# Attention outputs two query blocks at a time, and layer 2's modulation sums in layer 1's output projection

## The chip, the core and the metric

The kernel runs on one core of a Trainium2 chip. The metric is the device time of one execution in microseconds (us). Below, PE is the matrix engine, DVE, ACT and POOL are the vector, scalar and GpSimd engines, and SP is the engine whose queue issues most DMAs.

## What is computed

Two layers of a decoder trunk on 1024 tokens of width 1024. Each layer has a modulation of the conditioning vector, an input projection into three branches, and an output projection with a norm and a residual. Cut to what matters here:

```python
mod = jax.nn.silu(c) @ w_mod + b_mod                 # c: (1, D), w_mod: (D, 3 * D)
shift, scale, gate = jnp.split(mod, 3, axis=-1)
h = rmsnorm(x, g_pre) * (1.0 + scale[:, None]) + shift[:, None]
proj = h @ w_in
o_a = sliding_window_attention(a_q, a_k, a_v, sinks) * jax.nn.silu(a_g)   # 16 heads of 64, 4 groups of keys
...
mix = jnp.concatenate([o_a, o_b, o_c], axis=-1)
out = rmsnorm(mix @ w_out, g_post)
return x + gate[:, None] * out
```

Branch B is a gated linear attention and branch C a diagonal state-space model (S5) with a gated linear unit.

## The kernel before

Products run in two float32r parts, so that each weight tile is loaded raw (`wraw`, three buffers), rounded by ACT (`whi`) and its rest taken by DVE (`wlo`, L53), with four buffers for each part. The scheduler of the framework orders each engine's instructions by the order in which the program names them and by when their operands and buffers come free in its own estimate; each engine, and SP's queue of DMAs, then runs in that order, and an instruction that waits holds what is behind it.

A layer is emitted in stages: the input norm, the projections of branch B with the S5 tables, branch B, the attention stage, and the output projection. The function `attention` walks eight pairs of heads by eight blocks of 128 queries, 64 blocks a layer. Each block is a generator, `attn_block`, of three steps that run in three successive iterations: scores and softmax (PE L588, L589, DVE L594 and L603, ACT L599), transposes and split of the probabilities (L609, L53), and products with the values (L619, L620). The last step has one PSUM bank `po` a block. The upper half of its partitions is copied by ACT to `t2` (L622), DVE adds the halves head by head (L626), and for the first six pairs POOL multiplies the gate in (L629). For the last two pairs the sum goes straight to `M`, and the gate follows.

Between the blocks the same loop emits the S5 scans (16 batches, in the first 27 blocks; POOL works in each at L1316 and L1322, DVE at L1315 to L1326), queued projections, and one or two steps of an iterator `side`. In layer 1's attention `side` runs `mod_part` eight times: gate columns of layer 1, parts (0, 4) and (0, 5), and all six parts of layer 2, (1, 0) to (1, 5), where the first number is the layer counted from 0. A part is 512 columns; it has eight steps, each of which loads 128 rows into a `wraw` buffer and adds them, scaled by `c`, to an accumulator: 

```python
            if (l, j) > (1, 2):
                nc.gpsimd.tensor_scalar(...)
```

so that (1, 3) to (1, 5) are summed by POOL (L147, L150), the five others by DVE (L133, L135). A few products with ones then sum over the partitions (L159 or L175). The results of parts (1, 0) to (1, 3), shift and scale, are needed when layer 2's input is normed (`prenorm`); the others, the gates, in the output projection of their own layer.

PSUM has two pools: two banks `pj` for projections and six banks for all else. The function `out_proj` takes layer 1's tokens in groups of three, three and two tiles; for each of 16 slices of 128 rows of `w_out` it loads two weight tiles, splits them and the matching slice of `M` (`mhi`, `mlo`) and runs 18 products (L1472), with a bank for each token tile and half of the columns.

Of the kernel before, what the change touches and what calls it, by code (L numbers as in the profile page):

```python
# [13 lines left out]
F32 = mybir.dt.float32  # L14
# [10 lines left out]
P = 128  # L25
D = 1024
# [9 lines left out]
# parts of M at the end of a layer: heads of branch A in pairs, branch B, branch C  # L36
# [5 lines left out]
class Trunk:  # L42
# [7 lines left out]
    def split(self, hi, lo, src):  # L50
        """hi = src rounded to float32r, lo = src - hi (exact in float32r)."""
        self.nc.scalar.copy(hi, src)  # L52
        self.nc.vector.tensor_tensor(out=lo, in0=src, in1=hi.bitcast(F32), op=ALU.subtract)  # L53
# [31 lines left out]
    def queue(self, name, gen, units=4):  # L85
        """units of products in a generator whose first step is to load; units = 0: no such step."""
        self.q.append([name, gen, units, units > 0])

    def prefetch(self, n=0):
        """emit the loads of the queue's entry n ahead of its products."""  # L90
# [4 lines left out]
    def unit(self):  # L95
        """emit one unit of the queue; False if it is empty."""
# [18 lines left out]
    def finish(self, name=None):  # L115
        """emit the queue up to the end of the named entry, or all of it."""
# [7 lines left out]
    def rstd(self, ss, n, w=1):  # L124
        """(ss / n + EPS) ** -0.5 on a small tile, in place."""
# [12 lines left out]
    def mod_part(self, l, j):  # L138
        """512 columns at a time; j: shift 0, 1, scale 2, 3, gate * g_post 4, 5."""
        nc, i = self.nc, self.i  # L140
        cols = slice(j * 512, (j + 1) * 512)
        acc = self.w2("macc")
        for k in range(KD):
            w = self.wraw()[:, 0:512]
            nc.sync.dma_start(w, i["w_mod"][l, k * P:(k + 1) * P, cols])
            if (l, j) > (1, 2):
# [6 lines left out]
            yield  # L153
        if j < 4:
            bm = self.lp.tile([P, KD], F32, name="bm")
            nc.sync.dma_start(bm[:, 0:4], i["b_mod"][l, cols].rearrange("(k p) -> p k", p=P))
            pm = self.psum("pm")
# [24 lines left out]
    # ---- first layer's input: norm, transpose, modulation, split, by blocks of 256 columns; a_v grows with them  # L182
    def startup(self):
# [5 lines left out]
        # c, b_mod and g_pre with D on partitions  # L189
# [12 lines left out]
        def load(n):  # L202
            """256 rows of 512 columns for shift or scale."""
# [12 lines left out]
        # silu(c) = c * (1 + tanh(c / 2)) / 2  # L216
# [6 lines left out]
        # sums that grow side by side in a bank are one group, opened by a product with zeros  # L223
# [22 lines left out]
        # rows of w_mod whose products run on the tensor engine; the others are summed first  # L246
        direct = (((2, 5), (1, 2, 5)), ((2,), (5,)))

        def mods(b):
            """shift and scale of a half of the columns."""  # L250
# [27 lines left out]
        def prep(b, h):  # L278
            """half of the columns, half of the tokens."""
# [1322 lines left out]
```

## Time and profile before

| | |
|---|---|
| three runs | 1858.48, 1860.26 and 1860.9 us |
| median | 1860.26 us |
| profiled execution | its span is 1860.8 us; no time of its own stands beside it |
| PE busy | 94% of the span |
| DVE busy | 73% |
| ACT busy | 46% |
| POOL busy | 32% |
| mean granted clock of PE | 0.980 of full speed |

Shares are means over stages that differ. On the time axis from the span's start, layer 1's attention stage runs from about 386 to 777 us and layer 2's from about 1302 to 1671 us; layer 1's output projection starts at 777 us. A busy PE row includes the modelled end of each product, so a busy share near one does not by itself say that PE never waits.

### The profile page before, as it was taken

How to read it: one execution, taken by the hardware profiler on the slowest of the kernel's cores; microseconds unless marked ns; L12 is line 12 of the kernel's file. 1: busy time of each engine (PE TensorE's matmuls, PEld its weight loads, DVE VectorE, ACT ScalarE, POOL GpSimd, SP SyncE). 2: the span in 40 equal slices, each digit the busy share in tenths (PEclk: the TensorE clock that was granted, in tenths of full speed). 3: DMA queues.
4: the chain of work that ended last, by engine and by line, in shares of the span. 5: the costliest groups of instructions: out<-in, count | busy, mean ns of one | idle time of the engine just before them, and what ended most of it. 6: DMA issues, size and time to landing. Idle time of an engine off the chain costs nothing.

```text
span 1860.8 us, 28251 instructions
## 1 busy us (share of the span) xinstructions
PE 1749.4 (94%) x9403; PEld 1458.5 (78%) x9403; DVE 1353.2 (73%) x2975; ACT 859.7 (46%) x1973; POOL 589.0 (32%) x1005
## 2 busy tenths in 40 slices
PE   7999799999989989999998999999999899999998
PEld 5987688887777677788778878888878767878876
DVE  6986796579999798647676765954898978873534
ACT  5233333445556565446663242423555656642433
POOL 4279750212343454002217850401323511000100
PEclk7999999999999999999998999999999999999999
DMA  8143402235542322335464432222345111113342
GB/s 308 31 108 125 131 29 74 65 113 171 170 142 69 114 74 76 101 125 184 169 199 95 137 102 57 57 60 65 104 128 150 52 46 41 35 51 134 105 165 101
DMA packets 239385, 198.24 MB, mean 107 GB/s; under 512 B 49596, under 2 KB 195068, under 8 KB 239240
## 3 DMA queue, kind: packets, MB, share of 16 engines
q1 hardware_dynamic: 211640, 172.54, 30.9%
q10 hardware_dynamic: 25536, 16.80, 2.9%
q0 software_dynamic: 2064, 7.11, 1.0%
q8 instruction: 74, 1.21, 0.3%
q14 instruction: 71, 0.58, 0.1%
HBM read 163.13 MB, written 37.46 MB: 108 GB/s over the span
## 4 chain that ended last, share of the span: by engine, by line
PE 61%; DVE 21%; ACT 5%; issue 5%; POOL 4%; DMA 4%; SPq 0%; ACTq 0%; DVEq 0%; POOLq 0%
PE py L1472 14%; PE pj L387 9%; PE pj L389 9%; PE pj L388 9%; DVE wlo L53 2%; PE pj L1472 2%; PE pa L884 2%; PE pj L1370 2%; DVE p L594 2%; DVE pl L53 1%; PE pT L609 1%; PE pj L408 1%; PE pj L410 1%; PE pj L409 1%; DVE p L603 1%
## 5 line engine op out<-in xcount | busy, mean ns | idle before, releaser
L387 PE MATMUL pj<-H,whi 128*128 128x512 f32 x1088 | 442.8, 407 | 10.6 <-DVE M L1386 6.4
L389 PE MATMUL pj<-H,wlo 128*128 128x512 f32 x1088 | 431.7, 397 | 5.5 <-DVE wlo L53 5.5
L388 PE MATMUL pj<-H,whi 128*128 128x512 f32 x1088 | 431.0, 396 | 0.0
L53 DVE TENSOR_TENSOR wlo<-wraw,whi 128x512 fp32r<-128x512 f32 (+1 forms) x320 | 238.6, 765 | 87.2 <-ACT whi L52 86.5
L52 ACT CAST whi<-wraw 128x512 fp32r<-128x512 f32 (+1 forms) x320 | 191.4, 618 | 185.3 <-PE pj L388 108.9
L387 PEld LDWEIGHTS pj<-H,whi 128*128 128x128 f32 x1088 | 207.6, 191 | 56.4 <-DVE M L1386 7.2
L389 PEld LDWEIGHTS pj<-H,wlo 128*128 128x128 f32 x1088 | 207.1, 190 | 54.3 <-DVE wlo L53 7.4
L388 PEld LDWEIGHTS pj<-H,whi 128*128 128x128 f32 x1088 | 207.6, 191 | 40.9 <-issue 1.3
L599 ACT ACTIVATE p<-p,st 128x257 f32<-128x257 f32 (+1 forms) x256 | 125.7, 492 | 153.4 <-DVE st L594 133.4
L53 DVE TENSOR_TENSOR mlo<-M,mhi 128x384 fp32r<-128x384 f32 (+2 forms) x80 | 53.4, 675 | 141.8 <-ACT mhi L52 135.7
L1472 PE MATMUL py<-whi,mhi 128*128 128x512 f32 x448 | 142.4, 397 | 6.6 <-ACT whi L52 3.5
L1472 PE MATMUL py<-wlo,mhi 128*128 128x512 f32 x448 | 144.8, 396 | 0.6 <-DVE wlo L53 0.5
L1472 PE MATMUL py<-whi,mlo 128*128 128x512 f32 x448 | 143.3, 394 | 0.7 <-DVE mlo L53 0.7
L1493 POOL TENSOR_SCALAR yrs<-yss 128x1 f32<-128x1 f32 x16 | 6.7, 418 | 376.5 <-ACT junk L1489 375.4
L52 ACT CAST mhi<-M 128x384 fp32r<-128x384 f32 (+2 forms) x80 | 50.3, 634 | 158.4 <-PE pj L1472 92.7
L594 DVE CUSTOM_DVE_ANT_0 p<-sc,bias,sink 128x256 f32<-128x256 f32 (+1 forms) x256 | 111.4, 463 | 9.2 <-PE sc L589 8.1
L583 POOL COPY p<-sink 128x2 f32<-128x2 f32 x128 | 36.0, 283 | 220.9 <-PE pT L609 102.2
L1472 PEld LDWEIGHTS py<-whi,mhi 128*128 128x128 f32 x448 | 83.1, 188 | 28.9 <-ACT whi L52 6.7
L1472 PEld LDWEIGHTS py<-wlo,mhi 128*128 128x128 f32 x448 | 84.2, 188 | 22.9 <-DVE wlo L53 4.1
L1472 PEld LDWEIGHTS py<-whi,mlo 128*128 128x128 f32 x448 | 84.1, 188 | 20.0 <-DVE mlo L53 1.5
L410 PE MATMUL pj<-wlo,H 128*128 128x256 f32 (+1 forms) x320 | 92.9, 292 | 6.3 <-DVE wlo L53 6.3
L408 PE MATMUL pj<-whi,H 128*128 128x256 f32 (+1 forms) x320 | 93.6, 293 | 3.7 <-DVE hv L346 2.7
(380 smaller groups left out, 3931.8 us busy)
## 6 DMA issues: line engine op xcount, KB each, us to landing
wraw<-in_w_in_dram SPq DMA_DIRECT2D x160, 256.0 KB
wraw<-in_w_out_dram SPq DMA_DIRECT2D x160, 256.0 KB
wraw<-in_w_mod_dram SPq DMA_DIRECT2D x64, 256.0 KB
M<-s5tab SPq DMA_DIRECT2D x32, 256.0 KB
M<-s5turn SPq DMA_DIRECT2D x64, 128.0 KB
M<-in_w_mod_dram SPq DMA_DIRECT2D x10, 512.0 KB
s5tab<-O ACTq DMA_DIRECT2D x8, 512.0 KB
s5tab<-G ACTq DMA_DIRECT2D x8, 512.0 KB
```

Source lines behind the costliest of these rows:

```text
L52: self.nc.scalar.copy(hi, src)
L53: self.nc.vector.tensor_tensor(out=lo, in0=src, in1=hi.bitcast(F32), op=ALU.subtract)
L387: nc.tensor.matmul(pj, hi, hh, start=(k == 0), stop=False)
L388: nc.tensor.matmul(pj, hi, hl, start=False, stop=False)
L389: nc.tensor.matmul(pj, lo, hh, start=False, stop=(k == KD - 1))
L408: nc.tensor.matmul(pj[:, :N], hh, hi, start=(k == 0), stop=False)
L410: nc.tensor.matmul(pj[:, :N], hh, lo, start=False, stop=(k == KD - 1))
L594: nc.vector.tensor_tensor_reduce(out=p[:, h, 0:n], in0=sc[:, h * 256:h * 256 + n], in1=bias[:, h, o0:o0 + n], scale=-1.0, scalar=self.sink ...
L599: nc.scalar.activation(p[:, h, 0:n + 1], p[:, h, 0:n + 1], AF.Exp, bias=neg[:, h:h + 1], scale=-1.0, accum_out=den[:, h:h + 1])
L884: nc.tensor.matmul(pa[:, j * P:(j + 1) * P], X[:, c * P:(c + 1) * P], xq[:, :, c * 64:(c + 1) * 64], start=True, stop=True)
L1370: nc.tensor.matmul(pz, wg[:, k, :], self.M[:, MIX_C[k], ts_], start=(k == 0), stop=(k == 3))
L1472: self.nc.tensor.matmul(py[t, h], lhs, ws[h][w][:, 0, :], start=(n == 0 and first), stop=(n == N - 1 and last))
```

## The change

Blocks of queries are taken in twos. An even block's products go to the first half of bank `po` and stop there; the odd block's go to the second half, and then one copy of 64 x 512, two additions of 64 x 256 and one gate multiplication of 128 x 256 serve both. The bank is thus held from the even block's third step to the odd block's.

Modulation parts: layer 1's attention keeps (0, 4), (0, 5) and takes (1, 3) third; all three are summed by POOL, as `pool` is true by default. Parts (1, 0) and (1, 1) on DVE and (1, 2) on POOL run in layer 1's output projection, with raw tiles, accumulators and a PSUM bank of their own (`mraw`, two buffers for both chains; `macc`; `pj`). Parts (1, 4) and (1, 5) run on POOL in layer 2's attention, which had none. The diff also deletes comments; that is left out here.

```diff
-    def mod_part(self, l, j):
+    def mod_part(self, l, j, pool=True, room=None, bank="pm"):
...
-        acc = self.w2("macc")
+        acc = room.tile([P, 512], F32, name="macc") if room else self.w2("macc")
         for k in range(KD):
-            w = self.wraw()[:, 0:512]
+            w = room.tile([P, 512], F32, name="mraw", bufs=2) if room else self.wraw()[:, 0:512]
             nc.sync.dma_start(w, i["w_mod"][l, k * P:(k + 1) * P, cols])
-            if (l, j) > (1, 2):
+            if pool:
...
-            pm = self.psum("pm")
+            pm = self.psum(bank)
...
-        po = self.psum("po")
+        if b % 2 == 0:
+            self.po = self.psum("po")
+        po = self.po
+        dst = po[:, b % 2 * 256:b % 2 * 256 + 256]
         for kt in range(nk):
...
-        t2 = self.ap.tile([64, 256], F32, name="t2", bufs=1)
-        nc.scalar.copy(t2, po[64:128, 0:256])
-        m = self.M[:, MIX_A[pair], b * P:(b + 1) * P]
-        o = self.ap.tile([P, P], F32, name="o") if pair < 6 else m
+        if b % 2 == 0:
+            return
+        t2 = self.ap.tile([64, 512], F32, name="t2", bufs=1)
+        nc.scalar.copy(t2, po[64:128, :])
+        m = self.M[:, MIX_A[pair], (b - 1) * P:(b + 1) * P]
+        o = self.ap.tile([P, 2 * P], F32, name="o") if pair < 6 else m
...
+        side = [] if last else [
+            chain(*(self.mod_part(l + 1, j, False, self.sp, "pj") for j in range(2))),
+            self.mod_part(l + 1, 2, True, self.sp, "pj")]
...
+                if side:
+                    for f in (side[0], side[1], side[0])[:2 + n % 2]:
+                        next(f, None)
...
-            parts = [(0, 4), (0, 5), (1, 0), (1, 1), (1, 2), (1, 3), (1, 4), (1, 5)] if l == 0 else []
+            parts = [(0, 4), (0, 5), (1, 3)] if l == 0 else [(1, 4), (1, 5)]
```

How the instructions move is shown at three places. First, SP's queue of DMAs where layer 1's output projection begins (`wraw` are raw weights, `mraw` raw modulation weights, `gg` the gate, `x_sb` the residual). Before:

```order
L370 DMA wraw<-in_w_out_dram 128x512 x6
L1433 DMA gg<-gg_84 128x1024
L1478 DMA x_sb<-in_x_dram 128x1024 x2
L370 DMA wraw<-in_w_out_dram 128x512 x30
L1501 DMA xmid<-yn 128x1024
```

And now:

```order
L372 DMA wraw<-in_w_out_dram 128x512 x7
L1442 DMA gg<-gg_84 128x1024
L145 DMA mraw<-in_w_mod_dram 128x512 x2
L1494 DMA x_sb<-in_x_dram 128x1024
L145 DMA mraw<-in_w_mod_dram 128x512 x2
L372 DMA wraw<-in_w_out_dram 128x512 x2
L1494 DMA x_sb<-in_x_dram 128x1024
L145 DMA mraw<-in_w_mod_dram 128x512 x2
L372 DMA wraw<-in_w_out_dram 128x512 x2
L145 DMA mraw<-in_w_mod_dram 128x512 x2
L372 DMA wraw<-in_w_out_dram 128x512 x2
```

After the first seven weight loads, two modulation loads now stand ahead of every two weight loads, through twelve such rounds.

Second, POOL at the first S5 scans of layer 1's attention (`s5a<-s5a` and `s5a<-s5b` are the scans' two multiplications, `M<-M,o` the gate, `macc` the modulation sums). Before:

```order
L1316 TENSOR_TENSOR s5a<-s5a,M 128x256
L583 COPY p<-sink 128x2
L1322 TENSOR_TENSOR s5a<-s5b,M 128x256
L1316 TENSOR_TENSOR s5a<-s5a,M 128x256
L1322 TENSOR_TENSOR s5a<-s5b,M 128x256
L583 COPY p<-sink 128x2
L629 TENSOR_TENSOR M<-M,o 128x128
```

And now:

```order
L147 TENSOR_SCALAR wraw<-wraw,cc 128x512
L1325 TENSOR_TENSOR s5a<-s5a,M 128x256
L150 TENSOR_TENSOR macc<-macc,wraw 128x512
L585 COPY p<-sink 128x2
L1331 TENSOR_TENSOR s5a<-s5b,M 128x256
L1325 TENSOR_TENSOR s5a<-s5a,M 128x256
L147 TENSOR_SCALAR wraw<-wraw,cc 128x512
L150 TENSOR_TENSOR macc<-macc,wraw 128x512
L1331 TENSOR_TENSOR s5a<-s5b,M 128x256
L585 COPY p<-sink 128x2 x2
L638 TENSOR_TENSOR M<-M,o 128x256
```

Modulation work of two instructions now stands between the scans' multiplications, where POOL had none of it.

Third, DVE at the start of the output projection, in the change:

```order
L53 TENSOR_TENSOR mlo<-M,mhi 128x384 x3
L133 TENSOR_SCALAR macc<-mraw,cc 128x512
L53 TENSOR_TENSOR mlo<-M,mhi 128x384
L53 TENSOR_TENSOR wlo<-wraw,whi 128x512 x2
L135 SCALAR_TENSOR_TENSOR macc<-mraw,cc,macc 128x512
```

The sums of parts (1, 0) and (1, 1) stand between the splits of the weights and of `M`; before, the splits followed each other alone.

## Rows read from the trace of the kernel before

**Rows 1.** The page, part 1: busy time, share of the span, instructions.

```profile
PE 1749.4 (94%) x9403; PEld 1458.5 (78%) x9403; DVE 1353.2 (73%) x2975; ACT 859.7 (46%) x1973; POOL 589.0 (32%) x1005
```

**Rows 2.** Score reduction L594 by stretch: count, durations (min/median/max), first and last start.

```profile
L594 DVE CUSTOM_DVE_ANT_0 p<-sc,bias,sink x48: 340/478/485, 386.8 to 536.6; 128x256 f32<-128x256 f32 x42, 128x128 f32<-128x128 f32 x6
L594 DVE CUSTOM_DVE_ANT_0 p<-sc,bias,sink x80: 332/479/486, 542.9 to 759.3; 128x256 f32<-128x256 f32 x70, 128x128 f32<-128x128 f32 x10
L594 DVE CUSTOM_DVE_ANT_0 p<-sc,bias,sink x48: 342/478/485, 1302.5 to 1447.2; 128x256 f32<-128x256 f32 x42, 128x128 f32<-128x128 f32 x6
L594 DVE CUSTOM_DVE_ANT_0 p<-sc,bias,sink x80: 339/479/486, 1454.9 to 1653.3; 128x256 f32<-128x256 f32 x70, 128x128 f32<-128x128 f32 x10
```

**Rows 3.** Output projection's products L1472, layer 1 (without its last tiles), then layer 2.

```profile
L1472 PE MATMUL py<-whi,mhi x256: 387/395/505, 777.1 to 967.0; 128*128 128x512 f32 x128
L1472 PE MATMUL py<-whi,mhi x192: 388/393/502, 1671.1 to 1850.0; 128*128 128x512 f32 x192
```

**Rows 4.** Busy time by stretch: length, PE, PEld, DVE, ACT, POOL, PE clock, DMA, GB/s.

```profile
386.00:543.00 157.00, 147.04 (x850) 126.87 (x849) 147.61 (x409) 84.48 (x228) 47.59 (x82) 0.99 0.48 145
543.00:777.00 234.00, 217.48 (x1083) 171.93 (x1083) 196.82 (x526) 133.07 (x338) 88.97 (x133) 0.98 0.30 88
777.00:842.00 65.00, 64.62 (x278) 52.25 (x279) 30.47 (x50) 26.24 (x49) 0.00 (x0) 1.00 0.42 142
1302.00:1455.00 153.00, 145.22 (x845) 125.47 (x843) 137.36 (x387) 86.39 (x233) 49.01 (x84) 1.00 0.41 120
1455.00:1671.00 216.00, 207.92 (x1047) 164.63 (x1047) 174.25 (x499) 129.54 (x333) 40.40 (x85) 0.98 0.15 43
```

**Rows 5.** Modulation sums: DVE from 386 to 543 us; then POOL and PE, all.

```profile
L135 DVE SCALAR_TENSOR_TENSOR macc<-wraw,cc,macc x18: 722/746/753, 387.8 to 542.2; 128x512 f32<-128x512 f32 x18
L133 DVE TENSOR_SCALAR macc<-wraw,cc x3: 457/481/482, 431.5 to 541.7; 128x512 f32<-128x512 f32 x3
...
L150 POOL TENSOR_TENSOR macc<-macc,wraw x21: 1267/1287/2009, 631.1 to 729.9; 128x512 f32<-128x512 f32 x21
L159 PE MATMUL pm<-ones,macc x32: 164/250/250, 526.9 to 665.9; 128*128 128x1 f32 x32
```

**Rows 6.** Output of the blocks: additions, copy, gate, both layers.

```profile
L626 DVE TENSOR_TENSOR o<-po,t x192: 253/283/286, 401.6 to 1590.9; 64x128 f32<-64x128 f32 x192
L622 ACT COPY t<-po x128: 353/370/373, 399.5 to 1664.2; 64x256 f32<-64x256 f32 x128
L629 POOL TENSOR_TENSOR M<-M,o x96: 452/462/966, 402.7 to 1591.4; 128x128 f32<-128x128 f32 x96
```

**Rows 7.** Nearest operations with 256 or 512 columns, on DVE, ACT and POOL.

```profile
L1315 DVE TENSOR_TENSOR s5a<-pe,M x32: 413/422/425, 392.0 to 1447.6; 128x256 f32<-128x256 f32 x32
L52 ACT CAST ph<-pT x128: 365/587/593, 393.5 to 1660.2; 128x512 fp32r<-128x512 f32 x112, 128x256 fp32r<-128x256 f32 x16
L1316 POOL TENSOR_TENSOR s5a<-s5a,M x32: 725/742/989, 391.7 to 1444.2; 128x256 f32<-128x256 f32 x32
```

**Rows 8.** Instructions in time: start, us, engine, line; then all of L603.

```profile
718.74 0.70 POOL L147 TENSOR_SCALAR wraw<-wraw,cc 128x512 f32<-128x512 f32 x1
719.52 1.28 POOL L150 TENSOR_TENSOR macc<-macc,wraw 128x512 f32<-128x512 f32 x1
721.61 1.30 POOL L150 TENSOR_TENSOR macc<-macc,wraw 128x512 f32<-128x512 f32 x1
...
719.65 2.02 DVE L603 TENSOR_SCALAR p<-p,st 128x256 f32<-128x256 f32 x2
721.59 0.67 DVE L1409 SCALAR_TENSOR_TENSOR sgate<-sgate,pj 128x512 f32<-128x512 f32 x1
...
L603 DVE TENSOR_SCALAR p<-p,st x256: 261/350/1467, 388.6 to 1655.1; 128x256 f32<-128x256 f32 x112, 128x128 f32<-128x128 f32 x16
```

**Rows 9.** DVE's waits in layer 2's attention: who for whom, us, times, longest.

```profile
DVE s5a L1317 <- POOL s5a L1316: 3.3, 8, 0.5
```

**Rows 10.** Chain of waits: start, us, what.

```profile
627.55 2.67 DMA wraw<-in_w_mod_dram
...
942.85 4.34 DMA wraw<-in_w_out_dram
```

**Rows 11.** SP's issues of `w_out` from 783 to 801 us; DVE's weight splits there.

```profile
L370 SPq DMA_DIRECT2D wraw<-in_w_out_dram x10: 327/328/328, 783.4 to 800.7; - x10
...
786.88 1.30 DVE L53 TENSOR_TENSOR wlo<-wraw,whi 128x512 fp32r<-128x512 f32 x2
791.04 1.29 DVE L53 TENSOR_TENSOR wlo<-wraw,whi 128x512 fp32r<-128x512 f32 x2
```

More of the change, by code (lines that the diff above doesn't have):

```diff
@@ L153, in mod_part @@
             yield
+        if room:
+            yield
         if j < 4:
@@ L618, in attn_block @@
             sl = slice(kt * 256, (kt + 1) * 256)
-            nc.tensor.matmul(po[:, 0:256], v, ph[:, sl], start=(kt == 0), stop=False)
-            nc.tensor.matmul(po[:, 0:256], v, pl[:, sl], start=False, stop=(kt == nk - 1))
-        t2 = self.ap.tile([64, 256], F32, name="t2", bufs=1)
-        nc.scalar.copy(t2, po[64:128, 0:256])
-        m = self.M[:, MIX_A[pair], b * P:(b + 1) * P]
-        o = self.ap.tile([P, P], F32, name="o") if pair < 6 else m
+            nc.tensor.matmul(dst, v, ph[:, sl], start=(kt == 0), stop=False)
+            nc.tensor.matmul(dst, v, pl[:, sl], start=False, stop=(kt == nk - 1))
+        if b % 2 == 0:
[4 more added lines that the diff above has]
+        o = self.ap.tile([P, 2 * P], F32, name="o") if pair < 6 else m
+        heads = lambda t, h: t.rearrange("p (b h t) -> p b h t", b=2, h=2)[:, :, h, :]
         for h in range(2):
-            nc.vector.tensor_tensor(out=o[64 * h:64 * h + 64, :],
-                                    in0=po[0:64, h * P:(h + 1) * P], in1=t2[:, h * P:(h + 1) * P], op=ALU.add)
+            nc.vector.tensor_tensor(out=o[64 * h:64 * h + 64, :].rearrange("p (b t) -> p b t", b=2),
+                                    in0=heads(po[0:64, :], h), in1=heads(t2, h), op=ALU.add)
         if pair < 6:
```

## The prediction

> **What bounds the kernel now.** I read the page's busy shares first: PE is busy for 94% of the span and DVE for 73% [rows 1]. These are means over unlike stages, so the second step is the places that the change touches, by the first and last starts of one instruction. Layer 1's attention begins with its first score reduction at 386.8 us and ends where the output projection's first product starts, at 777.1; layer 2's runs from 1302.5 to 1671.1 [rows 2, 3]. That is 390.3 against 368.6 us for the same blocks, scans and projections: layer 1 takes 21.7 us more, and what it does more is the eight modulation parts. The trace of before thus holds its own comparison, and the forecast hangs on it.
>
> The score reductions split the surplus. The first three pairs are 48 reductions, and the fourth begins at 542.9 and at 1454.9 [rows 2]: 156.1 against 152.4 us there (3.7 more), 234.2 against 216.2 in the rest (18.0 more).
>
> Third, busy time by stretch [rows 4]. In the first three pairs, where the scans run, DVE is busy for 147.61 of 157 us in layer 1 and for 137.36 of 153 in layer 2. It is nearly full, but the 10.25 us that layer 1 has more cost only 3.7: each us of DVE work there costs 0.36 us of time. That is my rate for DVE work in these stages. PE is close behind (145.22 of 153), and this limits what a lighter DVE can return. In the output projection PE is busy for 64.62 of 65 us, DVE for half, POOL not at all: modulation hides there only while nothing delays PE's weights.
>
> **The change part by part.**
>
> A. Layer 1's pairs 3 to 7 lose all modulation: the last DVE parts, and the three POOL parts whose 21 additions run from 631.1 to 729.9 us [rows 5]. The price is the 18.0 us between the layers. I take -17, since some of it may be chance in how the two layers fall; the bounds are -18 and half, -9.
>
> B. The first three pairs lose 18 x 0.746 + 3 x 0.48 = 14.9 us of DVE sums [rows 5], and get about 21 steps on POOL, each 0.70 + 1.29 = 2.0 us [rows 5, 8]. These are not free to DVE. While POOL worked on such steps without a break, two multiplications L603 on DVE took 2.02 us together, where one alone has a median of 0.35; a gate operation L1409 that reads PSUM took 0.67 beside a full 1.30 us POOL addition [rows 8]. So an operation of one kind pays (1.3 us over one and a half steps, up to 0.9 a step) and others pay nothing. I take 0.4 a step: 8.4 us back, a net 6.5 us less on DVE, by 0.36 some -2.3. The scans' multiplications on POOL now stand behind modulation; DVE's wait for them is small now (3.3 us in eight waits [rows 9]), and I add 0.8. Sum -1.5; bounds -5 (the 14.9 at 0.36, nothing back) and +5 (0.9 a step, and some 3 us of waits).
>
> On this point the Trainium skill is stricter. Its page "SBUF — State Buffer", section "Who interferes with whom", says that DVE and GpSimd share a port pair as an exclusive lock for a whole instruction, where DVE has two SBUF inputs or runs in a two-port mode. The longer L603 and the untouched L1409 agree with it. Taken to its end it gives the slow rival below; by the rows the sum goes on with 0.4.
>
> C. Outputs of two blocks together, 32 times a layer. DVE: four additions of 0.283 become two. The nearest row for twice the columns from PSUM is L1315, 0.422, so 1.13 becomes 0.84: 0.29 x 32 = 9.2 us less a layer. ACT: two copies of 0.370 become one, near 0.587 (512 columns from PSUM), 4.9 us less. POOL: two gates of 0.462 become one of 0.742 (256 columns), 0.18 x 24 = 4.4 us less [rows 6, 7]. ACT and POOL have room, so only DVE's share counts: 9.2 x 0.36 = 3.3 a layer, for both -6. Bounds: 0, if the bank that is held longer makes PE wait, and -18.4, if DVE's time counts in full. PE's own products stay.
>
> D. Layer 2's attention gets parts (1, 4) and (1, 5) on POOL: 16 steps x 0.4 x 0.36 = 2.3, and 0.7 for the scans' waits, +3. Bounds 0 and +8 (0.9 a step is 5.2, and some 3 us of waits). Two gate products move along, at nothing.
>
> E. The 12 small products of parts (1, 0) to (1, 2) move into a stage that PE fills: 12 x 0.11 to 0.25 us [rows 5], +1.5 (1.3 to 3). The 16 sums on DVE, 12 us, have room in a stage in which DVE is idle for over 30 of 65 us.
>
> F. The 24 loads of these parts stand in SP's queue ahead of weight loads, two by two, and share two buffers. The next pair waits until both are used, and the weights queue behind it. A load that POOL uses takes 0.33 to issue and 2.67 to land [rows 10, 11], then 2.0 us of POOL: 5.0, where PE needs two weight tiles each 18 products; weights are split every 4.16 us (786.88 to 791.04 [rows 11]). DVE's loads take 0.33 + 2.67 + 0.75 = 3.75 and keep up. With twice the traffic a landing may take 3.2, so a POOL round takes 5.5 and loses 1.3. POOL uses eight of the 24 loads; where two in turn fall on one buffer the whole round is lost, elsewhere part of it. I count four to eight full losses, 5 to 10 us. Against this stands the lead: weights issued at 783.4 land near 786.1, PE needs them as its fourth slice, at 777.1 + 3 x 4.16 = 789.6 [rows 3, 11], and the split takes 0.65 on DVE and about as much on ACT before: some 2.2 us to spare, and for the pair's second tile, needed 4.16 later, some 6. What is left is 0 to 7; I take +3. With the landing of 4.34 of a busier stretch [rows 10] it would be +12, the upper bound.
>
> **Sum:** -17 - 1.5 - 6 + 3 + 1.5 + 3 = -17. Everything else keeps its instructions. The profiled execution's span is 1860.8, half a us above the median of the runs, 1860.26; the forecast is 1860.8 - 17 = **1844 us**.
>
> **The rivals.**
>
> 1. *DVE's time counts in full.* In the scans it is 94% to 95% busy, which speaks for it; that 10.25 us cost only 3.7 speaks against it. A -18, B -6.5, C -18.4, D +6.4, E and F +4.5: -32, 1829 us.
>
> 2. *The output projection starves* behind modulation loads: F is +12 in place of +3, 1853 us. For it: PE has no idle time there now, so any late weight shows at once. Against: the lead, and loads that land in 2.67.
>
> 3. *The change doesn't give what it says.* The bank is held for a block longer, PE waits for it and C is 0; B is 0, and half of A was never modulation's: -9 + 3 + 4.5 = -1.5, 1859 us. Against: six banks remain for at most two or three users at once.
>
> 4. *Slower: POOL's modulation holds DVE in the scans.* POOL gets 21 + 16 steps where DVE is fullest. If each held DVE for its whole 2.0 us, as the skill's lock would have it at worst, 37 x 2.0 x 0.36 = 26.6 would stand for the 5.3 that I count: +21, 1865 us. The forecast turns into a loss when a step costs over about 1.7 us of DVE, for 37 x 0.36 x (1.7 - 0.4) = 17. For it: L603 at three times its median. Against: the dense stretch shows at most 0.9, and L1409 nothing.
>
> **How the numbers follow.** The forecast's case, 1837 to 1851, gets 0.60; rival 1 0.12, rival 2 0.10, rival 3 0.10, rival 4 0.08. The range 1828 to 1858 takes in rivals 1 and 2 and the forecast's bounds, and leaves out rival 4 and part of 3. About 0.2%, 3.7 us, is what a measurement can tell from no change, so faster means below 1856.5: the forecast, rivals 1 and 2, 0.82. Within 0.2% is rival 3, 0.10; slower is rival 4, 0.08.
>
> **What would show it.** In the changed profile the two attention stages should take nearly the same time, each near 365 to 370 us, and layer 1's pairs 3 to 7 should take near 214 us (A). The pair additions should take 0.42 us, 128 in place of 256 (C). L603 should be longer beside POOL's sums in the first pairs, and by how much decides rival 4 (B, D). In the output projection PE's busy share in the first 65 us, and SP's waits for POOL's additions, decide F; if that first group of tiles takes over 72 us, rival 2 holds. The forecast is wrong if layer 1's attention stays over 380 us, or layer 2's goes over 376.

## The result, and the profile after

The changed kernel took 1882.8 us (median of four runs, 1881.81 to 1884.57), the one before 1860.58 beside it: a ratio of 1.0126, 95% interval [1.0113, 1.014]. The forecast was 1844, so the sign was wrong. The profiled execution of the changed kernel has a span of 1881.8 us, 21.0 more than before. Lines moved: the score reduction is now L596, the products of the output projection L1488, the scans' POOL multiplications L1325 and L1331.

The page's busy times, against [rows 1]: DVE works 33.9 us less, POOL 35.9 more.

```profile
PE 1753.2 (93%) x9403; PEld 1459.9 (78%) x9403; DVE 1319.3 (70%) x2823; ACT 847.8 (45%) x1909; POOL 624.9 (33%) x1002
```

The score reductions of the changed kernel by stretch (count; shortest, median and longest ns; first and last start), as [rows 2]:

```profile
L596 DVE CUSTOM_DVE_ANT_0 p<-sc,bias,sink x48: 343/478/486, 388.1 to 552.2; 128x256 f32<-128x256 f32 x42, 128x128 f32<-128x128 f32 x6
L596 DVE CUSTOM_DVE_ANT_0 p<-sc,bias,sink x80: 338/478/485, 558.8 to 755.7; 128x256 f32<-128x256 f32 x70, 128x128 f32<-128x128 f32 x10
L596 DVE CUSTOM_DVE_ANT_0 p<-sc,bias,sink x48: 343/479/485, 1310.6 to 1470.3; 128x256 f32<-128x256 f32 x42, 128x128 f32<-128x128 f32 x6
L596 DVE CUSTOM_DVE_ANT_0 p<-sc,bias,sink x80: 337/478/486, 1477.9 to 1674.9; 128x256 f32<-128x256 f32 x70, 128x128 f32<-128x128 f32 x10
```

The output projection's first token tiles (96 products of one kind a group of three tiles), two groups before, then two of the changed kernel:

```profile
L1472 PE MATMUL py<-whi,mhi x96: 390/394/501, 777.1 to 843.2; 128*128 128x512 f32 x96
L1472 PE MATMUL py<-whi,mhi x96: 388/394/482, 844.3 to 912.4; 128*128 128x512 f32 x96
```

```profile
L1488 PE MATMUL py<-whi,mhi x96: 386/393/506, 773.8 to 850.0; 128*128 128x512 f32 x96
L1488 PE MATMUL py<-whi,mhi x96: 387/394/483, 851.2 to 919.2; 128*128 128x512 f32 x96
```

Differences of first starts give the account. Layer 1's first three pairs take 170.7 us (388.1 to 558.8) and took 156.1: +14.6. Its pairs 3 to 7 take 215.0 (to 773.8) and took 234.2: -19.2. The first three tiles take 77.4 and took 67.2: +10.2. Layer 2's first three pairs take 167.3 and took 152.4: +14.9. These four make +20.5 of the 21.0. So the modulation left pairs 3 to 7 as forecast, and cost more at each of the three places that it went to.

Busy time by stretch of the changed kernel (columns as in [rows 4]): the first three pairs, the rest and the first tiles, then the first three pairs of layer 2.

```profile
388.00:559.00 171.00, 150.03 (x843) 129.75 (x842) 145.09 (x371) 85.62 (x222) 83.07 (x111) 0.96 0.47 138
559.00:774.00 215.00, 207.68 (x1060) 165.04 (x1059) 168.99 (x457) 125.06 (x312) 38.79 (x74) 0.99 0.15 43
774.00:851.00 77.00, 72.86 (x312) 55.60 (x312) 47.70 (x73) 28.70 (x56) 17.96 (x17) 1.00 0.63 207
1310.00:1478.00 168.00, 150.90 (x849) 129.66 (x848) 140.49 (x369) 85.36 (x222) 68.09 (x96) 0.96 0.43 129
```

In the first three pairs DVE is busy for 145.09 of 171 us: it works less than before and stands idle for 26 us in place of 9. It is not a full DVE that makes the stage longer. PE stands idle for 21 in place of 10, and its granted clock is 0.96 in place of 0.99. Who waits for whom there (us in total, times, longest; `s5a` are the scans' intermediate sums), before and after:

```profile
DVE s5a L1317 <- POOL s5a L1316: 0.8, 3, 0.4
PE py L1332 <- DVE s5a L1326: 6.2, 6, 1.8
```

```profile
POOL wraw L147 <- DMA wraw<-in_w_mod_dram: 13.7, 7, 2.9
DVE s5a L1326 <- POOL s5a L1325: 12.0, 4, 6.5
PE py L1341 <- DVE s5a L1335: 17.3, 8, 7.3
```

POOL waits for modulation loads, DVE waits for POOL's first scan multiplication, PE waits for the end of the scan. The timeline shows one such chain at the start of layer 2's attention (start, us, engine, line; in brackets the idle time before and what the profile takes for its releaser):

```profile
1316.35 0.69 POOL L147 TENSOR_SCALAR wraw<-wraw,cc 128x512 f32<-128x512 f32 x1 [3.79 <-DVE s5a L1324]
1317.13 1.29 POOL L150 TENSOR_TENSOR macc<-macc,wraw 128x512 f32<-128x512 f32 x1
1321.31 0.69 POOL L147 TENSOR_SCALAR wraw<-wraw,cc 128x512 f32<-128x512 f32 x1 [2.90 <-DMA wraw<-in_w_mod_dram]
1321.97 0.72 POOL L1325 TENSOR_TENSOR s5a<-s5a,M 128x256 f32<-128x256 f32 x1
1322.72 1.47 DVE L1326 TENSOR_TENSOR s5a<-s5a 128x256 f32<-128x256 f32 x1 [6.86 <-POOL s5a L1325]
1328.68 0.80 PE L1341 MATMUL py<-s5a,M 128*128 128x127 f32 x2 [7.66 <-DVE s5a L1335]
```

L1325 multiplies what ACT copies out of PSUM in L1322 and L1323, and the second copy ends at 1315.4. POOL stands at a modulation step then, whose load lands at 1316.1 (the profile names L1324 there, which the step does not read). L1325 comes behind it and behind half of the next one: 1.98 us of sums, 2.90 of waiting for the next load, 0.69 of the next step. DVE, in order too, idles for 6.86 us, and then PE for 7.66. PE pays a second time, as busy time by stretch around that stop shows (the columns of [rows 4], with the clock behind POOL's):

```profile
1315.00:1321.00 6.00, 6.00 (x33) 4.94 (x31) 0.64 (x3) 2.63 (x8) 1.98 (x2) 1.00 0.23 75
1321.00:1328.60 7.60, 0.02 (x1) 0.00 (x0) 5.80 (x12) 0.00 (x0) 5.87 (x8) 0.70 0.12 35
1328.60:1334.00 5.40, 5.32 (x21) 4.93 (x22) 5.17 (x18) 3.12 (x9) 2.22 (x3) 0.50 0.47 139
```

After standing for 7.6 us PE runs at half its clock (1.2 GHz, the lower of its two levels) for the next 5.4 us.

### The profile page after: what moved, and what is told of

Read it like the earlier page. It is cut to its first block, busy times and chain, and to the rows that moved or that the text cites. A ratio compares the mean times of both kernels' runs of the same rounds, so it can differ in the third digit from the quotient of the medians.

```text
span 1881.8 us, 28019 instructions
## 1 busy us (share of the span) xinstructions
PE 1753.2 (93%) x9403; PEld 1459.9 (78%) x9403; DVE 1319.3 (70%) x2823; ACT 847.8 (45%) x1909; POOL 624.9 (33%) x1002
## 5 line engine op out<-in xcount | busy, mean ns | idle before, releaser
L601 ACT ACTIVATE p<-p,st 128x257 f32<-128x257 f32 (+1 forms) x256 | 125.7, 493 | 176.6 <-DVE st L596 168.4
L1488 PE MATMUL py<-whi,mhi 128*128 128x512 f32 x448 | 144.0, 399 | 7.9 <-ACT whi L52 4.6
L1488 PE MATMUL py<-wlo,mhi 128*128 128x512 f32 x448 | 147.8, 401 | 1.2 <-DVE wlo L53 0.8
L1488 PE MATMUL py<-whi,mlo 128*128 128x512 f32 x448 | 144.0, 395 | 0.7 <-DVE mlo L53 0.7
L585 POOL COPY p<-sink 128x2 f32<-128x2 f32 x128 | 34.4, 270 | 293.8 <-PE pT L611 162.4
L596 DVE CUSTOM_DVE_ANT_0 p<-sc,bias,sink 128x256 f32<-128x256 f32 (+1 forms) x256 | 111.5, 463 | 20.1 <-PE sc L591 19.1
L1488 PEld LDWEIGHTS py<-whi,mhi 128*128 128x128 f32 x448 | 83.0, 188 | 31.5 <-ACT whi L52 9.7
L1488 PEld LDWEIGHTS py<-wlo,mhi 128*128 128x128 f32 x448 | 84.8, 189 | 26.9 <-DVE wlo L53 8.8
L1488 PEld LDWEIGHTS py<-whi,mlo 128*128 128x128 f32 x448 | 84.8, 190 | 19.6 <-DVE mlo L53 1.5
```

Of the source, the lines that this page charges most:

```text
L585: nc.gpsimd.tensor_copy(p[:, :, n], self.sink[:, h0:h0 + 2])
L596: nc.vector.tensor_tensor_reduce(out=p[:, h, 0:n], in0=sc[:, h * 256:h * 256 + n], in1=bias[:, h, o0:o0 + n], scale=-1.0, scalar=self.sink ...
L601: nc.scalar.activation(p[:, h, 0:n + 1], p[:, h, 0:n + 1], AF.Exp, bias=neg[:, h:h + 1], scale=-1.0, accum_out=den[:, h:h + 1])
L1488: self.nc.tensor.matmul(py[t, h], lhs, ws[h][w][:, 0, :], start=(n == 0 and first), stop=(n == N - 1 and last))
```

## The experiments

Below, "first three pairs" is layer 1's and layer 2's stretch from the first score reduction to that of the fourth pair, "pairs 3 to 7" the rest up to the output projection, "first tiles" the first group of three; all are differences of first starts in one profiled execution, as above. Ratios are to the kernel before, run on the same chip (medians of 1861.7 to 1864.0 there).

| kernel | time, us | ratio, interval | first three pairs | pairs 3 to 7 | first tiles |
|---|---|---|---|---|---|
| before | 1860.58 | | 156.1, 152.4 | 234.2, 216.2 | 67.2 |
| changed | 1882.8 | 1.0126 [1.0113, 1.014] | 170.7, 167.3 | 215.0, 215.3 | 77.4 |
| pairing alone | 1865.36 | 1.0018 [0.9999, 1.0037] | 153.8, 149.5 | 239.1, 215.2 | 67.2 |
| moves alone | 1885.89 | 1.0133 [1.0112, 1.0155] | 172.5, 169.4 | 215.7, 215.8 | 77.1 |
| DVE sums in attention | 1854.07 | 0.9955 [0.994, 0.9971] | 156.0, 153.8 | 215.0, 215.3 | 78.7 |
| steps from block 4 | 1880.11 | 1.0101 [1.0072, 1.0129] | 171.1, 165.4 | 217.4, 215.0 | 78.6 |
| steps from block 28 | 1894.28 | 1.0172 [1.0145, 1.0198] | 148.5, 148.1 | 249.9, 237.9 | 78.2 |
| no loads | 1862.9 | 0.9999 [0.9979, 1.002] | 162.3, 155.2 | 215.7, 214.8 | 79.4 |
| small sums | 1848.51 | 0.9928 [0.9904, 0.9952] | 154.8, 154.7 | 215.5, 215.2 | 78.7 |
| loads by POOL | 1916.48 | 1.0283 [1.0245, 1.032] | 192.6, 178.8 | 214.5, 215.0 | 78.0 |
| own raw tile | 1881.18 | 1.0099 [1.0057, 1.0142] | 173.2, 163.8 | 214.4, 215.2 | 79.3 |
| block 28, loads by POOL | 1892.9 | 1.0167 [1.0109, 1.0224] | 148.5, 148.6 | 250.9, 232.8 | 77.7 |
| projection on DVE | 1880.23 | 1.0085 [1.0062, 1.0108] | 171.9, 166.7 | 215.0, 215.5 | 73.9 |
| four raw tiles | 1878.25 | 1.0084 [1.0054, 1.0115] | 172.2, 166.9 | 216.2, 215.3 | 75.5 |
| all sums on DVE | 1855.39 | 0.9947 [0.9925, 0.9968] | 157.9, 155.2 | 215.3, 215.1 | 72.9 |
| all in attention, DVE | 1854.16 | 0.9948 [0.9932, 0.9964] | 153.7, 155.3 | 225.1, 214.9 | 67.2 |
| all on DVE, own tile | 1860.53 | 0.9999 [0.9981, 1.0018] | 162.1, 157.3 | 215.6, 215.1 | 72.2 |

The stage columns repeat well where the code is the same: layer 2's pairs 3 to 7 take 214.8 to 215.8 us in the fourteen kernels whose steps do not reach them, the first tiles 77.1 to 79.4 in the ten that leave them as in the changed kernel, and layer 1's first three pairs 170.7 to 172.2 in three. Smaller differences than these say nothing.

**Which half of the change.** Pairing alone takes the moves back, by the edit below; moves alone keeps one bank, copy and gate a block.

```diff
-        side = [] if last else [
+        side = [] and [
...
-            parts = [(0, 4), (0, 5), (1, 3)] if l == 0 else [(1, 4), (1, 5)]
-            self.attention(l, (s for a in parts for s in self.mod_part(*a)))
+            parts = [(0, 4), (0, 5), (1, 0), (1, 1), (1, 2), (1, 3), (1, 4), (1, 5)] if l == 0 else []
+            self.attention(l, (s for a in parts for s in self.mod_part(*a, a > (1, 2))))
```

> The changed kernel's pairing of blocks alone; all eight modulation parts stand where the kernel before had them (five on DVE, three on POOL, all in layer 1's attention). Theory Q (order: in the changed kernel the first S5 multiplication on POOL stands behind eight modulation steps that load one at a time, and DVE and PE wait for it): without those steps the first three pairs take 150 to 157 us in both layers, as before, and the whole 1850 to 1860 us. Theory L (POOL's modulation slows DVE through a shared resource, step by step): the same numbers. Theory B (a bank held for two blocks makes PE wait): the first three pairs stay near 171 and 167 us as in the changed kernel, and the whole is 1880 us or more.

> The changed kernel's modulation moves alone; each block has its own bank, copy, additions and gate as before. Q and L: the first three pairs stay at 165 to 171 us in both layers, the output projection's first three tiles at 75 to 79 us (67 before), the whole 1878 to 1892 us. B: the first three pairs return to 152 to 158 us, the whole below 1865 us.

Pairing gives 2.3 and 2.9 us in the first three pairs and in layer 2's rest 1.0; in layer 1's rest, where modulation runs as before, it takes 4.9 more. As a whole it cannot be told from no change, and misses the 1850 to 1860 us expected. The moves alone are as slow as the whole change. So the bank held for two blocks (theory B) is not the cause; the moves are.

**Which engine.** The sums of both attention stages go to DVE, in the same places.

```diff
-            self.attention(l, (s for a in parts for s in self.mod_part(*a)))
+            self.attention(l, (s for a in parts for s in self.mod_part(*a, False)))
```

> The changed kernel with the five parts in the two attention stages summed by DVE instead of POOL, in the same places of the program. Q: the first scan is free again; first three pairs 153 to 160 us in both layers, the whole 1853 to 1863 us (the output projection keeps its 10 us). L: the same direction, as POOL has no steps there. B: no change against the changed kernel, 1880 us.

The stages fall back by 14.7 and 13.5 us, and the time is below both kernels. A step works DVE, the fuller engine, for 0.75 us, and yet costs less time than on POOL. So it is POOL's steps in these stages that cost; what remains is how.

**Where in the stage.** The steps start with block 4, behind the first scan.

```diff
-                for _ in range(2 if n % 6 == 0 else 1):
+                for _ in range((2 if n % 6 == 0 else 1) if n >= 4 else 0):
```

> The changed kernel with the attention's modulation steps begun four blocks later, still on POOL and still within the scans, so that no step stands ahead of the first two scans' multiplications. Q: most of the first pair's 10 to 12 us comes back in each layer; first three pairs 154 to 162 us, the whole 1858 to 1870 us. L: the same 24 and 16 steps slow DVE by as much as before, first three pairs 165 to 172 us, the whole 1878 to 1886 us.

The narrow form of theory Q fell: the sum stays, the loss only moves on to the later pairs, and the numbers are those of theory L. (All 24 and 16 steps now lie in the first three pairs; in the changed kernel four in each layer stand ahead of the first score reduction, which leaves 20 and 12.) The loss also has another form here. In layer 1's first three pairs DVE's wait for POOL's first multiplication, and two of its own operations (busy, mean ns, idle), are

```profile
DVE s5a L1326 <- POOL s5a L1325: 4.9, 10, 1.2
L605 DVE TENSOR_SCALAR p<-p,st 128x256 f32<-128x256 f32 (+1 forms) x48 | 20.2, 462 | 0.5
L1329 DVE TENSOR_TENSOR_SCAN s5b<-rho,s5a 128x128 f32<-128x128 f32 x32 | 16.4, 544 | 0.2
```

The wait is 4.9 us in place of 12.0, and DVE is busy for 151.93 us in place of 145.09: its operations are longer. The means of the two were 346 and 413 ns in the kernel before.

So the next question was whether scans are needed for the loss at all; with 28 in place of 4 the steps come after the last one.

> The changed kernel, but the modulation steps in both attention stages begin with block 28 (after the last S5 scan) in place of block 0; they stay on POOL, with the same loads. Theory Q2 (POOL's steps cost because the scans stand among them on POOL and DVE: without a scan to hold, a step is free): the first three pairs fall from 170.7 to about 153 and from 167.3 to about 150 us, as where nothing or only DVE sums stand there, pairs 3 to 7 stay at 215 to 218, and the time falls by 28 to 34 us to 1849 to 1855. Theory L2 (each POOL step slows DVE by its port wherever it stands; 1.0 us of time a step): the first three pairs fall as above, but pairs 3 to 7 rise by as much, 24 and 16 us, to 239 and 231, and the time stays near 1880.

The first three pairs come out at 148.5 and 148.1 us, the measure for this stage without any modulation. But pairs 3 to 7 pay more than the scans did: 249.9 and 237.9 in place of 215, about 1.4 us for each of the 24 and 16 steps. So theory Q2 fell, and theory L2's 1.0 us a step was too little. The rows on ACT in layer 1 (who for whom, us, times, longest):

```profile
ACT whi L52 <- DMA wraw<-in_w_in_dram: 17.9, 2, 11.1
ACT ge L1360 <- POOL ge L1359: 13.1, 7, 4.1
```

Two holders show: input weights that arrive late behind modulation loads, and POOL's part of the S5 gate. To tell them apart, POOL issues the loads into a tile of its own, so that SP's queue no longer sees them (here and in the other kernels with a tile of their own, `o` has one buffer, which is left out below):

```diff
-            w = room.tile([P, 512], F32, name="mraw", bufs=2) if room else self.wraw()[:, 0:512]
-            nc.sync.dma_start(w, i["w_mod"][l, k * P:(k + 1) * P, cols])
+            w = room.tile([P, 512], F32, name="mraw", bufs=2) if room else self.ap.tile([P, 512], F32, name="mraw", bufs=1)
+            (nc.sync if room else nc.gpsimd).dma_start(w, i["w_mod"][l, k * P:(k + 1) * P, cols])
```

> The changed kernel, with the modulation steps of the attention stages begun at block 28, after the scans, and their loads issued by POOL into a raw tile of their own. It tells apart why the late steps cost 34.9 and 22.8 us in pairs 3 to 7. Theory S (there by SP: the input projection's weights stand behind modulation loads whose raw tile POOL still holds): pairs 3 to 7 fall from 249.9 to 215 to 224 and from 238.0 to 215 to 220 us, and the time is 1846 to 1856. Theory H (POOL's own waits hold the gates and the gelu behind it, there too): they stay at 235 to 265 and 228 to 245.

The waits for `w_in` fall to 1.9 us, and the stage stays long (250.9 and 232.8), as theory H had it. POOL's own queue holds it:

```profile
POOL mraw L147 <- DMA mraw<-in_w_mod_dram: 35.3, 16, 3.1
ACT p L601 <- POOL p L585: 20.4, 5, 7.8
ACT ge L1360 <- POOL ge L1359: 18.2, 8, 5.9
```

L585 is POOL's copy of the sink into each block's scores, 0.19 us long in the median, and every exponent L601 on ACT needs it. POOL was 32% busy in the kernel before, but it has an operation on the path of every block.

**Load or sum.** One kernel keeps POOL's arithmetic and leaves seven of eight loads out; the other keeps all loads and cuts the sums to 16 columns (the multiplication in the same way as the addition below). Neither computes the whole modulation.

```diff
-            w = room.tile([P, 512], F32, name="mraw", bufs=2) if room else self.wraw()[:, 0:512]
-            nc.sync.dma_start(w, i["w_mod"][l, k * P:(k + 1) * P, cols])
+            if room or k == 0:
+                w = room.tile([P, 512], F32, name="mraw", bufs=2) if room else self.wraw()[:, 0:512]
+                nc.sync.dma_start(w, i["w_mod"][l, k * P:(k + 1) * P, cols])
+            else:
+                w = acc
```

> The changed kernel, but in the attention stages only the first step of a modulation part loads its weights; the other seven repeat the two POOL operations of a step on the accumulator itself, in the same shapes. This leaves out seven eighths of these parts' weights, so the modulation is not the reference's. POOL's arithmetic stays, its waits for loads and their places in SP's queue go. Without loads to wait for, the scheduler places a part's steps closer together. Theory A (the 2.0 us of POOL arithmetic a step, which hold the scans' POOL multiplications and lengthen DVE's operations): the first three pairs stay at 163 to 171 and 160 to 167 us. Theory W (POOL stands at the head of its queue for a load of 2.9 us, and the raw tiles hold SP's queue): they fall to 154 to 158 and 150 to 154.

```diff
+                c = slice(0, 16 if k and not room else 512)
...
-                    nc.gpsimd.tensor_tensor(out=acc, in0=acc, in1=w, op=ALU.add)
+                    nc.gpsimd.tensor_tensor(out=acc[:, c], in0=acc[:, c], in1=w[:, c], op=ALU.add)
```

> The changed kernel, but in the attention stages POOL's two operations of a modulation step take 16 of the 512 columns (the first step of each part stays whole). This leaves out most of these sums, so the modulation is not the reference's. Every load, its place in SP's queue and POOL's order of instructions stay as in the changed kernel; of the 2.0 us of arithmetic a step some 0.2 should be left. Theory A (the arithmetic costs): the first three pairs fall from 170.7 to 153 to 158 and from 167.3 to 149 to 154 us. Theory W (the waits for the loads cost, with POOL's and SP's queues behind them): they stay above 164 and 161. Between these, the two share it, and the part that each has is read from this run and the one without loads.

The waits of DVE and PE in layer 1's first three pairs, without loads, then with small sums:

```profile
DVE s5a L1329 <- POOL s5a L1328: 5.0, 4, 3.8
PE py L1344 <- DVE s5a L1338: 13.1, 8, 5.1
```

```profile
DVE s5a L1327 <- POOL s5a L1326: 1.6, 4, 0.4
PE py L1342 <- DVE s5a L1336: 4.6, 4, 1.9
```

Over the 148.5 and 148.1 of a stage without modulation, sums alone cost 13.8 and 7.1, loads alone 6.3 and 6.6, both together 22.2 and 19.2. These hold different numbers of steps, as the scheduler puts some ahead of the first score reduction: without loads a whole part stands there, which leaves 16 and 8, and with small sums 19 and 11 are left. By the step, sums alone cost 0.86 and 0.89 us, loads alone 0.33 and 0.60, both 1.11 and 1.60, so that the parts come near the whole (1.19 and 1.49). (Without loads an addition reads one tile twice and takes 1.04 us in place of 1.29, so the sums are priced a little low.) Neither theory holds alone; the arithmetic has the larger part. A load still waits where the sums are small (20.5 us of POOL's time in layer 1), but POOL is through with it at once, and DVE waits for 1.6 us only.

**POOL's queue or SP's.** The kernel whose loads POOL issues, with the steps in their first places, turns the theories against each other.

> The changed kernel, but in the attention stages the modulation loads are issued by POOL itself into one raw tile of their own (and o has one buffer); SP's queue and the three raw weight tiles no longer see them, and POOL waits for every load. Theory S (the cost comes by SP: weights and S5 tables late behind modulation loads that wait for a raw tile): the first three pairs fall from 170.7 to 155 to 162 and from 167.3 to 150 to 158 us. Theory H (the cost comes by POOL: it stands at a step that waits for its load, and the scans' multiplications behind it wait too): POOL now stands some 3 us in every step, so the first three pairs stay or rise, 168 to 190 in both layers.

It rises by 21.9 and 11.5 us, as H alone expected, in layer 1 past the 190 us it had. POOL, DVE and PE in layer 1's first three pairs:

```profile
POOL mraw L147 <- DMA mraw<-in_w_mod_dram: 33.8, 16, 3.0
DVE s5a L1326 <- POOL s5a L1325: 29.0, 4, 14.5
PE py L1341 <- DVE s5a L1335: 35.2, 8, 13.3
```

SP's queue has no modulation load in this stage, and the stage is the longest of all: what adds the time is that POOL stands for a load with the scans behind it. With one raw tile of their own but SP's queue (the diff above, `nc.sync` kept), POOL waits and sums in turns:

> The changed kernel, but the modulation loads of the attention stages have one raw tile of their own (and o one buffer); they stay in SP's queue and POOL sums them. Theory V (the modulation takes the three raw tiles from the weights): the first three pairs fall from 170.7 and 167.3 to 153 to 160 us. Theory H (POOL stands for a load, then sums for 2.0 us, and the scans' multiplications wait behind): with one tile every load starts only after the sum before it, so the first three pairs stay or rise, 168 to 185 us.

173.2 and 163.8: taking the weights' raw tiles out of it gives nothing in layer 1 and 3.5 us in layer 2. Theory V falls as the main cause.

**The output projection.** Part (1, 2) on DVE, then four raw tiles.

```diff
-            self.mod_part(l + 1, 2, True, self.sp, "pj")]
+            self.mod_part(l + 1, 2, False, self.sp, "pj")]
```

> The changed kernel, but part (1, 2), the one that POOL sums in layer 1's output projection, is summed by DVE; POOL has no modulation there. Theory R (POOL's round: a raw tile that POOL uses comes free only after 2.0 us of sums, and since both chains share two raw tiles, the loads behind it and the weights behind those wait): the first three token tiles, 77.4 us in the changed kernel and 67.3 before, take 68 to 71, and the time falls by 7 to 9 us, to about 1874. Theory T (the 24 loads of 256 KB themselves, in SP's queue ahead of the weights, cost it, whoever sums): the first three tiles stay at 76 to 79 and the time stays within 2 us of the changed kernel's. Both leave the attention stages at 386 and 383 us.

```diff
-            w = room.tile([P, 512], F32, name="mraw", bufs=2) if room else self.wraw()[:, 0:512]
+            w = room.tile([P, 512], F32, name="mraw", bufs=4) if room else self.wraw()[:, 0:512]
...
-        yn = sp.tile([P, D], F32, name="yn", bufs=3)
+        yn = sp.tile([P, D], F32, name="yn", bufs=2)
```

> The changed kernel, but with four raw tiles for the modulation loads of layer 1's output projection in place of two (and two in place of three buffers yn). POOL still sums part (1, 2). Theory R (the two raw tiles: a load waits until POOL or DVE is through with a tile, and the weights wait behind it in SP's queue): the first three token tiles fall from 77.4 to 70 to 73 us. Theory T (traffic and the small products themselves): they stay at 76 to 79.

Both fall short of R: 73.9 and 75.5, where 67.2 is the measure; the second also gives up 1.5 us in the second group. The rows of the changed kernel from 774 to 851 us:

```profile
SPq L145 <- POOL macc L150: 17.8, 6, 4.1
PE pj L161 <- DVE macc L135: 2.2, 1, 2.2
L161 PE MATMUL pj<-ones,macc x24: 166/251/271, 809.1 to 842.7; 128*128 128x1 f32 x24
```

SP does wait for POOL's sums. But PE also waits once at the head of its queue for DVE's last sum, and the small products are 24. By the starts of PE's products, of the 10.2 us 2.6 are the small products, 2.4 the stop before the first of them, and 5.0 lie in some 25 steps of 0.3 to 0.9 us between two main products, where 0.23 is usual. With part (1, 2) on DVE these last are 2.5 us; with four raw tiles they are 5.7, and the stop is gone. So each theory has a part.

**Versions.** All modulation on DVE, in the places of the change (the edits above for DVE's sums in both stages and for the four raw tiles together), or all of it in the attention stages:

> The changed kernel, but all modulation sums on DVE, in the places that the change gives them, and four raw tiles in the output projection (two buffers yn). If POOL's steps are the cost in the attention stages, these take 371 and 369 us as with DVE sums before; if the output projection loses by two raw tiles and POOL's sums, its first three tiles take 70 to 72 us, if by traffic and small products 74 or more. Time 1842 to 1849 us, under both kernels.

```diff
-        side = [] if last else [
+        side = [] and [
...
-            parts = [(0, 4), (0, 5), (1, 3)] if l == 0 else [(1, 4), (1, 5)]
-            self.attention(l, (s for a in parts for s in self.mod_part(*a)))
+            parts = [(0, 4), (0, 5), (1, 0), (1, 1), (1, 2), (1, 3)] if l == 0 else [(1, 4), (1, 5)]
+            self.attention(l, (s for a in parts for s in self.mod_part(*a, False)))
```

> Paired blocks, all modulation sums on DVE, six parts in layer 1's attention and two in layer 2's, none in the output projection. The first three pairs should take 156 and 154 us; the output projection's first three tiles 67 as before. Open are layer 1's pairs 3 to 7 with 24 DVE steps: at the 0.2 to 0.3 us that a DVE step costs in the first three pairs 220 to 222 us, and the time 1845 to 1849; at the 0.7 that it has by itself 232, and the time 1857.

The two and the first version with DVE sums have the same ratio within their intervals, 0.995: some 9 us under the kernel before, and less than expected (1842 to 1849 us). Where parts (1, 0) to (1, 2) stand matters little, once DVE sums them: in pairs 3 to 7 22 steps cost 9.8 us (225.1 to 215.3), in the output projection 24 cost 5.7. The first three pairs are 4.2 us shorter in the former, with 21 steps for 19; why is not shown (the two kernels with 19 lie 1.9 apart). An own raw tile (the edit from above, with DVE) was to recover what DVE's steps still cost:

> All modulation sums on DVE in the places that the change gives them, with four raw tiles in the output projection (two buffers yn), and one raw tile of their own in the attention stages (o with one buffer). Where the steps' loads took the weights' raw tiles, the 5 us a layer that DVE sums still cost go: the first three pairs take 150 to 154 us and the time is 4 to 8 us under the same without own tiles. Where DVE's own 0.75 us a step is what costs, they stay at 155 to 158 and the time does not change.

It does not; with one tile DVE itself waits for loads, and the stage gets longer.

## Why the prediction was wrong

Both of its signs of being wrong came: layer 1's attention took 385.7 us and layer 2's 382.6. Term by term:

**A** held: -19.2 in layer 1's pairs 3 to 7 for -17, and -18.5 with the moves alone.

**B failed, in its smallest term.** The price of DVE's slowing was right for this kernel: 21 steps at 0.4 us were to be 8.4 us. Measured kind by kind (the mean of an operation, less its mean in the same stage of the kernel with steps from block 28, which has no modulation there, times its count) DVE's operations are 9.0 us longer in all, 0.45 for each of the 20 steps there. The groups of lines in layer 1's first three pairs (busy, mean ns, idle) before and after show two of the operations that grew:

```profile
L603 DVE TENSOR_SCALAR p<-p,st 128x256 f32<-128x256 f32 (+1 forms) x48 | 14.6, 346 | 0.2
L1320 DVE TENSOR_TENSOR_SCAN s5b<-rho,s5a 128x128 f32<-128x128 f32 x32 | 12.2, 413 | 0.0
```

```profile
L605 DVE TENSOR_SCALAR p<-p,st 128x256 f32<-128x256 f32 (+1 forms) x48 | 17.8, 412 | 0.5
L1329 DVE TENSOR_TENSOR_SCAN s5b<-rho,s5a 128x128 f32<-128x128 f32 x32 | 14.3, 475 | 0.1
```

They grow by 3.2 and 2.1 us. The term that failed is "I add 0.8" for the scans' multiplications that now stand behind modulation. DVE's wait for them grew by 11.2 us, from 0.8 to 12.0 (the 3.3 of [rows 9] is layer 2's), and PE's for the scan by 11.1. PE is also busy for 3.0 us longer for about the same products (150.03 against 147.04), at a lower mean clock. These 14.1 are about the stage's 14.6. With pairing's -2.3 taken out, B was +16.9 where the sum has -1.5 and its upper bound +5; the moves alone have +16.4.

Neither of the two prices is fixed. With the steps from block 4 the wait is 4.9 us, but DVE's operations are longer by 16.5 us in layer 1 and 10.4 in layer 2, 0.69 and 0.65 a step, and the stage lasts as long. So the loss by POOL's steps is shown; how much of it is POOL's queue and how much are DVE's longer operations depends on where the steps stand, and stays open.

**The rate** of 0.36 us per us of DVE work does not carry over: it was taken from work that DVE does in its own queue, and says nothing of an engine that others wait for. For DVE's own steps, 0.75 us each, it would give 0.27 a step. The 21 steps of pairing alone cost 5.3 us in layer 1 (153.8 over 148.5), 0.25 a step; the 11 in layer 2 with DVE sums cost 5.7 (153.8 over 148.1), 0.52. It fits the first and is half of the second.

**C** was 3.3 us a layer: with pairing alone the first three pairs gave 2.3 and 2.9 and layer 2's rest 1.0, but layer 1's rest took 4.9, and the whole stays within what a measurement can tell. Where those 4.9 us come from is not shown.

**D failed** by the same term: 0.7 for the waits. Together with layer 2's half of C it came to +14.9, so D was +17.8 (with pairing's -2.9 taken out), where the sum has +3 and the upper bound is +8. DVE's wait for POOL's first multiplication there is 11.0 us, for 3.3 before; and only 12 of the 16 steps lie in that stretch.

**E** counted 12 products, and there are 24: eight a part, as the 32 for four parts in [rows 5] say. **F** was +3, with 12 as its upper bound; both together came to 10.2 for 4.5. Of these the small products are 2.6; 5.0 are late main products, which F had at 3, and 2.4 a stop for DVE's last sum, which neither term had. The first tiles took over 72 us, so rival 2 held here.

With the measured terms the sum comes out: -19.2 + 14.6 + 10.2 + 14.9 = +20.5.

**Rival 4** had the sign, at 0.08, the right place, and a part of the mechanism. It let POOL hold DVE's instructions for up to 2.0 us a step through a shared port. In the changed kernel they were longer by 0.45 us a step in layer 1 and 0.43 in layer 2 (5.2 us for 12), DVE's busy time fell and its idle time grew. The Trainium skill's page "SBUF — State Buffer", section "Who interferes with whom", has DVE and GpSimd lock each other out of a shared port pair for a whole instruction, where DVE has two SBUF inputs or runs in a two-port mode. The trace agrees in kind: L605 and L1329 get longer, an L1326 takes 1.47 us in the timeline above, and the score reductions, which read PSUM, keep their 478 ns. It does not bear out the size of the worst case: the most that any kernel here shows is 0.8 us a step. But it is no small part of what sums cost without loads: there DVE's operations are 8.8 and 6.3 us longer, where the stages lose 13.8 and 7.1, and with small sums they are not longer at all (-1.0 and 0.0). No run here separates the port's share from that of POOL's queue.

**What the trace of before had shown.** The surplus of layer 1's pairs 3 to 7 was taken in one piece, as DVE's and POOL's together. By pairs it says more; the score reductions of pairs 6 and 7, layer 1 and then layer 2, and POOL's additions in layer 1's pair 6:

```profile
L594 DVE CUSTOM_DVE_ANT_0 p<-sc,bias,sink x16: 332/476/484, 677.9 to 718.1; 128x256 f32<-128x256 f32 x14, 128x128 f32<-128x128 f32 x2
L594 DVE CUSTOM_DVE_ANT_0 p<-sc,bias,sink x16: 343/478/486, 724.8 to 759.3; 128x256 f32<-128x256 f32 x14, 128x128 f32<-128x128 f32 x2
L594 DVE CUSTOM_DVE_ANT_0 p<-sc,bias,sink x16: 342/480/483, 1582.8 to 1614.7; 128x256 f32<-128x256 f32 x14, 128x128 f32<-128x128 f32 x2
L594 DVE CUSTOM_DVE_ANT_0 p<-sc,bias,sink x16: 343/476/484, 1620.1 to 1653.3; 128x256 f32<-128x256 f32 x14, 128x128 f32<-128x128 f32 x2
L150 POOL TENSOR_TENSOR macc<-macc,wraw x10: 1273/1292/2009, 685.8 to 724.5; 128x512 f32<-128x512 f32 x10
```

Pair 6 took 46.9 us in layer 1 and 37.3 in layer 2: 9.6 more, with no DVE step in it and ten additions on POOL, about 1 us a step. That is near the price that the changed kernel paid for the 20 and 12 steps in its first three pairs (1.1 and 1.6). Pair 5 argued against it: it lost nothing with eight additions.

## What to carry to other kernels

An operation moved to an idle engine is priced by how long it stands at the head of that engine's queue, its wait for a load included, and by what stands behind it; the engine's busy share says nothing of that. It is priced also by what it does to its neighbours' operations (here DVE's, 0.4 to 0.8 us longer a step). Look for the short operations on the idle engine that others need (here a scan's multiplication and a 0.19 us copy in every block). And where the trace holds a stretch with the moved work and one without, compare them in the finest pieces that it allows before a price is set.

## What was not expected of the hardware

A stop of PE can cost more than its length: after 7.6 us without work the granted clock was 0.50 for 5.4 us, and in the stage's mean 0.96 where the same stage with DVE sums has 1.00.
